# A two-layer decoder trunk on one core: projection units by halves of features, an earlier values product, and output pairs in another order

## The chip, the core and the metric

The kernel runs on one core of one Trainium2 chip, with float32 inputs and outputs. The metric is the time on the device in microseconds (us) of one execution. Its engines are TensorE (PE, matmuls), VectorE (DVE), ScalarE (ACT), GpSimd (POOL) and SyncE (SP, which issues the loads). Each engine works through its own instructions in order and waits where an operand isn't ready.

## The reference

The trunk has two layers over one sequence of 256 tokens with 1024 features. A layer is a half-step SwiGLU FFN, a token mixer and another half-step FFN; each reads a normed and modulated input and adds to x.

```python
def modulate(h, shift, scale):
    return h * (1 + scale[:, None, :]) + shift[:, None, :]
def hybrid_mixer(h, ...):
    proj = h @ w_in
    c_q, c_kv, k_pe, gate_b, gate_c, val = jnp.split(proj, offs, axis=-1)
    q = (rms_norm(c_q, q_a_norm) @ w_uq).reshape(B, S, N_HEADS, QK_NOPE_DIM + QK_ROPE_DIM)
    kv = (rms_norm(c_kv, kv_a_norm) @ w_ukv).reshape(B, S, N_HEADS, QK_NOPE_DIM + V_HEAD_DIM)
    ...
    attn = causal_attention(q_full, k_full, v).reshape(B, S, ATTN_WIDTH)
    conv = gate_b * causal_short_conv(gate_c * val, conv_w)
    merged = jnp.concatenate([rms_norm(attn, attn_out_norm), rms_norm(conv, conv_out_norm)], axis=-1)
    return merged @ w_o
for l in range(DEPTH):
    mod = jnp.split(c_act @ w_ada[l] + b_ada[l], N_MOD, axis=-1)
    h = modulate(rms_norm(x, ffn1_norm[l]), mod[0], mod[1])
    x = x + FFN_RESIDUAL * (1 + mod[2])[:, None, :] * swiglu(h, ffn1_w_gu[l], ffn1_w_down[l])
    h = modulate(rms_norm(x, mix_norm[l]), mod[3], mod[4])
    y = hybrid_mixer(h, ...)
    x = x + (1 + mod[5])[:, None, :] * y
    h = modulate(rms_norm(x, ffn2_norm[l]), mod[6], mod[7])
    x = x + FFN_RESIDUAL * (1 + mod[8])[:, None, :] * swiglu(h, ffn2_w_gu[l], ffn2_w_down[l])
return rms_norm(x, final_norm)
```

D_FF is 2816, the projection of the mixer has 2208 columns, there are 8 heads, and both groups (attention, convolution) are 512 wide.

## The kernel before

x lies on the chip, transposed: eight tiles x[0] to x[7] of 128 features by 256 tokens. A float32 product is made from three products of a shorter type: every operand is split into a high and a low part, and mm3 (line 287 is the line of all its matmuls) multiplies high by high, high by low and low by high. An mm3 is so three matmuls and takes one 128x128 weight tile and one feature tile.

**Weights** come as chunks of 1 MB (16 tiles of 128x128), in one fixed order on SP's queue. Each chunk has three buffers in rings of three: `raw` (the load), `hi` (ACT, line 262) and `lo` (DVE, line 265). In the mixer the splits go in four cuts of 128x512, in the FFNs in two of 128x1024. A load is issued when the `raw` buffer of three chunks ago has been split. Ahead of each chunk stand **modulation rows**, `ada`, of 0.5 MB each in a ring of four: one DVE instruction (line 189) reduces a row to one column of `mod`.

**Input of a sub-layer.** When a down projection, or the mixer's output, has finished an output tile m, DVE adds it to x[m] (`residual`, line 394, with a gate column from `mod`), and `put` scales it: ACT writes the high part of u[m] (line 351), DVE the low part (line 357), ACT squares x[m] (line 318) and DVE adds the square to `acc` (line 322). `shifts` splits the shift columns once eight of them are there. The norm's factor r comes later, from a sum over `acc` by a matmul with ones (`rstd`, lines 338 to 344), so products start on u before r is known and are scaled by r when they leave PSUM.

**The mixer** is a list of units, `ORDER`. K, Q, P (latents of kv, q and the rest), c (convolution) and d (its gate) are units of projection: a group of four units uses one chunk and one PSUM tile with two outputs, i = 0 and 1, over the eight features. In the kernel before, unit n of a group makes output n // 2 over features 0 to 3 (n even) or 4 to 7 (n odd). X is the sum for r; L, Z the latent norms; N, V, v the keys and values; q, s, t, a (0 to 3) are, for a pair of heads, queries, scores, the transposition of the probabilities, and the values product. n and m are the norms of the attention and of the convolution group; each ends in eight tiles `mr` that feed the output projection's halves A and B, of two chunks each (A0, A1, B0, B1). A unit w loads and splits the next chunk ahead of its use. B finishes pairs of output tiles (g, i odd); after each pair come residuals and puts for FFN2, whose first unit follows.

**What sets the order.** In the mixer PE and SP run as the list is written. For ACT and DVE a scheduler puts the instructions in an order by priority: `due(t)` sets it to a clock, which counts the matmuls emitted so far, plus t, and `SLACK` holds t for each kind of unit. A larger t puts the work later, if something else is ready. In the FFNs all engines go by this priority. `acc` in `out` is the pair of PSUM tiles of the output; `acc` in `Stat` the sum of squares.

Of the kernel before, what the change touches and what calls it, by code (L numbers as in the profile page):

```python
# [18 lines left out]
P = 128  # L19
L = 2  # L20
D = 1024
S = 256
KD = D // P
# [15 lines left out]
ENGS = {'p': mybir.EngineType.PE, 's': mybir.EngineType.SP, 'v': mybir.EngineType.DVE, 'a': mybir.EngineType.Activation}  # L39
MAN = 'sp'  # L40
SM_ACT = 2
ORDER = ("K K K X K Q Q P Q Q P P L c c c P c N Z V v q0 q1 s0 q2 c c c c t0 s1 a0 q3 c c c t1 c a1 s2 s3 c c c c t2 d d a2 t3 d d a3 "
         "d n w d w d d A A A w m A A w A A A B B B B B B B B").split()
WIN = dict(K=0, Q=1, P=2, c=3, d=7)
WO = dict(A=0, B=2)
SLACK = {'B': 6000, 'K': -2000, 'L': -4000, 'N': 0, 'P': 6000, 'Q': 0, 'V': 1000, 'X': 6000, 'Z': -4000, 'a': -4000, 'c': 6000, 'd': 0, 'm': 6000, 'n': 0, 'q': 2000, 's': -6000, 't': -4000}
CUTS = 4
GUARD = ('m',)
MIX_SPLIT, MIX_ADA = 2000, 2000
# [70 lines left out]
def trunk(ctx: ExitStack, tc, x_d, c_d, pos_d, small_d, cst_d, ada_d, gu1_d, dn1_d, win_d, up_d, wo_d, gu2_d, dn2_d, out_d):  # L120
# [25 lines left out]
    x = one.tile([P, KD, S], F32, name="x")  # L146
# [4 lines left out]
    uL, uH = u[:, :, 0:S], u[:, :, S:]  # L151
# [59 lines left out]
    for l in range(L):  # L211
# [4 lines left out]
        n = {}  # L216
# [64 lines left out]
    def due(t):  # L281

        tc.cur_priority = int(clock[0] + t)
# [75 lines left out]
    class Pre:  # L359
# [20 lines left out]
            nc.scalar.activation(hcol, sh, AF.Copy)  # L380
            nc.vector.tensor_tensor(lcol, sh, f32(hcol), ALU.subtract)

        def put(self, k):
            g = self.scale(k)
            hi_of(uH[:, k, :S], x[:, k, :], g)
            lo_of(uL[:, k, :], uH[:, k, :S], x[:, k, :], g)
            self.stat.add(x[:, k, :])


    def residual(src, m, l, sub, f, halves=False):  # L390
# [177 lines left out]
    def mixer(l, pre, nxt):  # L568
        mf = one.tile([P, NJ, S], F32, tag="aH", name=nm("mf"))
        mr = one.tile([P, NJ, S], F32R, tag="aL", name=nm("mr"))  # L570
        ckv, cq, conv, V, K = mf[:, 0:2], mf[:, 2:5], mf[:, 5:9], mf[:, 9:13], mf[:, 13:21]
# [32 lines left out]
        def proj(t, evac):  # L604

            n = seen[t] = seen.get(t, -1) + 1
            if n % 4 == 0:
                open_[t] = chunk(), ps_tile()
            w, pt = open_[t]
            i = n % 4 // 2  # L610
            for k in range(n % 2 * 4, n % 2 * 4 + 4):
                mm3(pt[:, i, :], w, i * KD + k, uH[:, k, :], uL[:, k, :], k == 0, k == KD - 1, 2)
            if n % 4 == 3:
                due(SLACK[t])
                evac(scaled(pt))
# [163 lines left out]
        def out(t):  # L779
            n = seen[t] = seen.get(t, -1) + 1  # L780
            half = "AB".index(t)
            zH, zL = ((atH, atL), (cvH, cvL))[half]
            g, i = divmod(n, 4)
            if not acc:
                acc.extend((ps_tile(), ps_tile()))
            if i == 0:
                open_[t] = chunk()
            w = open_[t]
            steps = [(m, i) for m in range(4)] if half == 0 else [(m, k) for k in range(i % 2 * 2, i % 2 * 2 + 2) for m in
                                                                  (i // 2 * 2, i // 2 * 2 + 1)]  # L790
            for m, k in steps:
                m += 4 * g
                dst = acc[m // 2 % 2][:, g, (m % 2) * S:(m % 2 + 1) * S]
                mm3(dst, w, m % 4 * 4 + k, zH[:, k, :], zL[:, k, :], half == 0 and k == 0 and m % 2 == 0, half == 1 and k == 3)
            if half == 1 and i % 2 == 1:
                due(SLACK["B"])
                for q in (i - 1, i):
                    m = 4 * g + q
                    residual(acc[m // 2 % 2][:, g, (m % 2) * S:(m % 2 + 1) * S], m, l, 1, 1.0)
                    nxt.put(m)  # L800
                    if m == 5:
                        nxt.shifts()

        do = dict(K=lambda: proj("K", kv_evac), Q=lambda: proj("Q", q_evac), P=lambda: proj("P", qk_evac),
                  c=lambda: proj("c", conv_evac), d=lambda: proj("d", gate_evac), X=lambda: pre.stat.rstd(r, t=SLACK["X"]), L=kv_norm, N=keys, Z=q_norm,
                  V=lambda: values(0), v=lambda: values(1), n=lambda: head_norm("n", sat, attn, O_AN, atH, atL),
# [97 lines left out]
def _layout(a):  # L904
    g = {}
    g["x"] = np.ascontiguousarray(a["x"][0].T.reshape(KD, P, S).transpose(1, 0, 2))
    g["c"] = np.ascontiguousarray(a["c"])
    g["pos"] = np.ascontiguousarray(np.broadcast_to(a["positions"][0].reshape(8, 32), (16, 8, 32)).reshape(P, 32))
    cols = []
    for l in range(L):  # L910
        for name in ("b_ada", "ffn1_norm", "mix_norm", "ffn2_norm", "q_a_norm", "kv_a_norm"):
            cols.append(a[name][l].reshape(-1, P).T)
        for j in range(3):
            cols.append(a["conv_w"][l, j].reshape(-1, P).T)
        for name in ("attn_out_norm", "conv_out_norm"):
            cols.append(a[name][l].reshape(-1, P).T)
    cols.append(a["final_norm"].reshape(-1, P).T)
    cols.append(_const_cols())
    g["small"] = np.ascontiguousarray(np.concatenate(cols, axis=1))
    g["cst"] = _consts()  # L920
    wt = a["w_ada"].transpose(0, 2, 1).reshape(L * NA, P, D)
    g["ada"] = np.ascontiguousarray(wt[[l * NA + t for l, t in ADA_ORDER]])
    for f in (1, 2):
        t = _tiles(a[f"ffn{f}_w_gu"]).reshape(L, KD, 2, NJ, P, P)
        w = t.transpose(0, 3, 4, 1, 2, 5).reshape(L, NJ, P, CH)
        if f == 1:
            head = w[0, :8].reshape(8, P, 8, 2, P).transpose(2, 1, 0, 3, 4).reshape(1, 8, P, CH)
            w = np.concatenate([np.concatenate([head, w[:1, 8:]], axis=1), w[1:]], axis=0)
        g[f"gu{f}"] = np.ascontiguousarray(w)
        t = _tiles(a[f"ffn{f}_w_down"]).transpose(0, 2, 1, 3, 4).reshape(L, 11, 16, P, P)  # L930
        g[f"dn{f}"] = np.ascontiguousarray(t.transpose(0, 1, 3, 2, 4).reshape(L, 11, P, CH))
    w = a["w_in"]
    kv, kpe, q = w[:, :, QR:QR + KVR], w[:, :, QR + KVR:QR + KVR + 32], w[:, :, :QR]
    sw = np.concatenate([kpe[:, :, 16:], kpe[:, :, :16]], axis=2)
    parts = [kv, q, sw, sw, kpe, kpe]
    o = QR + KVR + 32
    for i, s in [(i, s) for i in range(4) for s in (1, 2)] + [(i, 0) for i in range(4)]:
        parts.append(w[:, :, o + s * CW + i * P:o + s * CW + (i + 1) * P])
    t = _tiles(np.concatenate(parts, axis=2))
    t = t.transpose(0, 2, 1, 3, 4).reshape(L, 9, 16, P, P)  # L940
    g["win"] = np.ascontiguousarray(t.transpose(0, 1, 3, 2, 4).reshape(L, 9, P, CH))
    uk = a["w_ukv"].reshape(L, 2, P, H, 128)
    nope = uk[..., :64].reshape(L, 2, P, 4, P).transpose(0, 2, 3, 1, 4).reshape(L, P, 1024)
    v = uk[..., 64:].reshape(L, 2, P, 512).transpose(0, 2, 1, 3).reshape(L, P, 1024)
    uq = a["w_uq"].reshape(L, 3, P, H, 96)
    uq = np.concatenate([uq, uq[..., 80:96], uq[..., 64:80]], axis=-1)
    uq = uq.transpose(0, 2, 3, 1, 4).reshape(L, P, 24 * P)
    g["up"] = np.ascontiguousarray(np.concatenate([nope, v, uq], axis=2))
    t = _tiles(a["w_o"]).reshape(L, 2, 4, KD, P, P)
    t = t.transpose(0, 1, 3, 2, 4, 5).reshape(L, 4, 16, P, P)  # L950
    g["wo"] = np.ascontiguousarray(t.transpose(0, 1, 3, 2, 4).reshape(L, 4, P, CH))
    return g
# [21 lines left out]
```

## Time and profile before

| | |
|---|---|
| median of three runs | 999.11 us (999.49, 997.51, 999.11) |
| the profiled execution, its own time | 1002.27 us |
| its span, first to last instruction | 1000.5 us |
| mean granted clock of PE | 0.994 |
| PE busy | 977.1 us, 98% of the span |
| DVE busy | 854.1 us, 85% |
| ACT busy | 581.3 us, 58% |
| chain that ended last, share of PE | 78% |

Names of tiles are those of the program, without their numbers: `u` is the input of a sub-layer, `mf` and `mr` the mixer's tiles, `ps` a PSUM tile, `raw`, `hi`, `lo` a chunk. "SPq" is SP's DMA issue. A row of the timeline has the start, the duration, engine, line, operation, output <- inputs, shape and count; brackets hold the idle time ahead of it and what ended it.

### The profile page before, as it was taken

What the parts mean: (1) busy time and instruction counts of PE and PEld (TensorE: products, weight loads), DVE (VectorE), ACT (ScalarE), POOL (GpSimd) and SP (SyncE); (2) the same over time, 40 slices, a digit from 0 to 9 for tenths busy, and PEclk for the clock granted to TensorE, in tenths of its full rate; (3) what the DMA queues carried; (4) which work ended last, traced back from release to release, by engine and by line L of the source; (5) the groups of instructions that cost most, each with busy time, mean ns of one, the idle gap of its engine ahead of it and who ended that gap; (6) DMA issues with size and microseconds to landing.
All of it is one profiled execution on the core that took longest, in us unless ns stands there. A gap on an engine that the chain in (4) does not pass through costs nothing.

```text
span 1000.5 us, 16812 instructions
## 1 busy us (share of the span) xinstructions
PE 977.1 (98%) x6560; PEld 898.1 (90%) x6560; DVE 854.1 (85%) x1598; ACT 581.3 (58%) x1010; POOL 8.0 (1%) x27
## 2 busy tenths in 40 slices
PE   9999999999999999999999999998999999999996
PEld 7999998899989988888998888888998998888885
DVE  5899999999999998988899878877799999766653
ACT  4465544467856755654486555543687676656541
POOL 0000110000000000000000000000000000000000
PEclk9999999999999999999999999998999999999998
DMA  9999998874746687877768777776355547655531
GB/s 348 376 361 340 336 320 324 311 282 154 275 178 253 234 318 253 301 267 291 270 219 324 279 258 283 277 255 214 124 217 193 200 171 290 215 178 201 173 122 43
DMA packets 47007, 250.78 MB, mean 251 GB/s; under 512 B 5504, under 2 KB 5824, under 8 KB 26576
## 3 DMA queue, kind: packets, MB, share of 16 engines
q1 hardware_dynamic: 46224, 248.81, 68.3%
q8 instruction: 51, 0.84, 0.3%
q10 hardware_dynamic: 288, 0.65, 0.2%
q0 software_dynamic: 416, 0.25, 0.1%
q14 instruction: 28, 0.23, 0.1%
HBM read 248.59 MB, written 1.10 MB: 250 GB/s over the span
## 4 chain that ended last, share of the span: by engine, by line
PE 78%; DVE 11%; DMA 7%; issue 1%; ACT 1%; SPq 0%; DVEq 0%; ACTq 0%
PE ps L287 78%; DMA ada<-in_ada 6%; DVE lo L265 5%; DVE ada L189 1%; DVE x L394 1%; DMA raw<-in_gu 1%; DVE acc L322 1%; DVE u L357 1%; PE ps L731 1%; DVE mr L355 1%; ACT hi L262 0%; DMA cb<-in_c 0%; DVE nt L594 0%; ACT mr L351 0%; DVE mf L767 0%
## 5 line engine op out<-in xcount | busy, mean ns | idle before, releaser
L287 PE MATMUL ps<-u,hi 128*128 128x256 f32 (+2 forms) x2464 | 599.8, 324 | 6.5 <-ACT u L351 3.7
L287 PE MATMUL ps<-u,lo 128*128 128x256 f32 (+1 forms) x1664 | 470.1, 283 | 1.1 <-DVE lo L265 1.1
L287 PEld LDWEIGHTS ps<-u,hi 128*128 128x128 f32 x2464 | 413.5, 190 | 46.4 <-ACT u L351 4.3
L265 DVE TENSOR_TENSOR lo<-raw,hi 128x1024 fp32r<-128x1024 f32 (+2 forms) x384 | 394.8, 1046 | 41.4 <-ACT hi L262 40.9
L262 ACT ACTIVATE hi<-raw 128x1024 fp32r<-128x1024 f32 (+2 forms) x384 | 338.3, 912 | 113.4 <-PE ps L287 48.9
L287 PEld LDWEIGHTS ps<-u,lo 128*128 128x128 f32 x1664 | 315.9, 190 | 1.4 <-DVE lo L265 1.4
L287 PE MATMUL ps<-a,hi 128*128 128x512 f32 (+1 forms) x792 | 248.6, 372 | 1.4 <-DVE a L355 1.4
L189 DVE CUSTOM_DVE_ANT_0 ada<-ada,cb,small 128x1024 f32<-128x1024 f32 x144 | 183.1, 1280 | 33.4 <-DMA ada<-in_ada 32.8
L287 PE MATMUL ps<-a,lo 128*128 128x256 f32 x704 | 197.9, 281 | 0.0
L287 PEld LDWEIGHTS ps<-a,hi 128*128 128x128 f32 x792 | 143.0, 189 | 29.8 <-DVE a L355 1.7
L287 PEld LDWEIGHTS ps<-a,lo 128*128 128x128 f32 x704 | 133.2, 189 | 0.0
L351 ACT ACTIVATE a<-cc 128x256 fp32r<-128x256 f32 x88 | 36.3, 415 | 68.0 <-DVE cc L413 56.3
L287 PE MATMUL ps<-mr,hi 128*128 128x256 f32 x384 | 70.6, 285 | 0.0
L351 ACT ACTIVATE u<-x,gs 128x256 fp32r<-128x256 f32 x40 | 20.3, 507 | 84.6 <-DVE x L394 84.6
L287 PEld LDWEIGHTS ps<-mr,hi 128*128 128x128 f32 x384 | 60.2, 192 | 0.8 <-issue 0.3
L287 PE MATMUL ps<-mr,lo 128*128 128x256 f32 x192 | 54.3, 283 | 0.0
L394 DVE SCALAR_TENSOR_TENSOR x<-ps,gate,x 128x256 f32<-128x256 f32 x76 | 35.9, 480 | 19.2 <-PE ps L287 18.5
L355 DVE TENSOR_TENSOR a<-cc,a 128x256 fp32r<-128x256 f32 x88 | 37.0, 422 | 16.0 <-ACT a L351 15.8
L412 ACT ACTIVATE cc<-g 128x256 f32<-128x256 f32 x54 | 22.5, 418 | 41.5 <-DVE g L411 41.5
L411 DVE TENSOR_TENSOR g<-ps,g 128x512 f32<-128x512 f32 x54 | 37.0, 685 | 0.7 <-ACT g L410 0.6
L287 PEld LDWEIGHTS ps<-mr,lo 128*128 128x128 f32 x192 | 36.8, 191 | 0.0
L410 ACT ACTIVATE g<-ps 128x512 f32<-128x512 f32 x54 | 31.2, 578 | 0.0
(121 smaller groups left out, 568.4 us busy)
## 6 DMA issues: line engine op xcount, KB each, us to landing
raw<-in_gu SPq DMA_DIRECT2D x87, 1024.0 KB, 5.8
ada<-in_ada SPq DMA_DIRECT2D x144, 512.0 KB, 6.2
raw<-in_dn SPq DMA_DIRECT2D x44, 1024.0 KB, 5.2
raw<-in_win SPq DMA_DIRECT2D x18, 1024.0 KB, 5.7
raw<-in_wo SPq DMA_DIRECT2D x8, 1024.0 KB, 4.8
raw<-in_up SPq DMA_DIRECT2D x2, 1024.0 KB, 5.9
raw<-in_up SPq DMA_DIRECT2D x2, 768.0 KB, 4.4
raw<-in_up SPq DMA_DIRECT2D x4, 384.0 KB, 3.1
```

What stands on the lines that cost most here:

```text
L189: nc.vector.tensor_tensor_reduce(out=a, in0=a, in1=cb, scale=1.0, scalar=sm(l, t), op0=ALU.mult, op1=ALU.add, accum_out=mods[l][:, t:t + 1])
L262: nc.scalar.activation(hi[:, zs[q]], raw[:, zs[q]], AF.Copy)
L265: nc.vector.tensor_tensor(lo[:, zs[q]], raw[:, zs[q]], f32(hi[:, zs[q]]), ALU.subtract)
L287: nc.tensor.matmul(dst, a, b, **kw)
L322: nc.vector.tensor_tensor(self.acc, self.acc, t, ALU.add)
L351: nc.scalar.activation(dH, src, AF.Copy, scale=scale)
L355: nc.vector.tensor_tensor(dL, src, f32(dH), ALU.subtract)
L357: nc.vector.scalar_tensor_tensor(dL, src, scale, f32(dH), ALU.mult, ALU.subtract)
L394: nc.vector.scalar_tensor_tensor(x[:, m, :], s, g, x[:, m, :], ALU.mult, ALU.add)
L410: nc.scalar.activation(t2, pg[:, :, :S], AF.Copy)
L411: nc.vector.tensor_tensor(t2, pg[:, :, S:], t2, ALU.add)
L412: nc.scalar.activation(sg, t2[:, 0, :], AF.Silu)
```

## The change

It has three parts.

1. **Projection by halves of features.** Unit n of a group now makes output n % 2 over features 0 to 3 (n = 0, 1) or 4 to 7 (n = 2, 3). The weights are rearranged on the host so that cut n of the chunk is still the one that unit n uses. The list begins K K Q Q K X K Q Q, where it began K K K X K Q Q P Q Q.
2. **The last values product** a3 moves ahead of a gate unit: t3 d a3 d d n in place of t3 d d a3 d n. The unit w that followed n and d, the first of four early loads, is left out; three remain, so that chunk B1 is taken when it is used.
3. **Output pairs.** Both residuals of a pair come first, then both scalings and splits, then the shifts (after the third pair), and last, with a due time of their own (`y`, 5000), the squares and their sum. `SLACK` of B goes from 6000 to 1500, and to 0 for the last pair.

```diff
-ORDER = ("K K K X K Q Q P Q Q P P L c c c P c N Z V v q0 q1 s0 q2 c c c c t0 s1 a0 q3 c c c t1 c a1 s2 s3 c c c c t2 d d a2 t3 d d a3 "
-         "d n w d w d d A A A w m A A w A A A B B B B B B B B").split()
+ORDER = ("K K Q Q K X K Q Q P P P L c c c P c N Z V v q0 q1 s0 q2 c c c c t0 s1 a0 q3 c c c t1 c a1 s2 s3 c c c c t2 d d a2 t3 d a3 "
+         "d d n d w d d A A A w m A A w A A A B B B B B B B B").split()
-SLACK = {'B': 6000, ...
+SLACK = {'B': 1500, 'y': 5000, ...
-        def put(self, k):
+        def put(self, k, add=True):
             g = self.scale(k)
             hi_of(uH[:, k, :S], x[:, k, :], g)
             lo_of(uL[:, k, :], uH[:, k, :S], x[:, k, :], g)
-            self.stat.add(x[:, k, :])
+            if add:
+                self.stat.add(x[:, k, :])
...
-            i = n % 4 // 2
-            for k in range(n % 2 * 4, n % 2 * 4 + 4):
-                mm3(pt[:, i, :], w, i * KD + k, uH[:, k, :], uL[:, k, :], k == 0, k == KD - 1, 2)
+            i, h = n % 2, n % 4 // 2
+            for k in range(4 * h, 4 * h + 4):
+                mm3(pt[:, i, :], w, 4 * (n % 4) + k % 4, uH[:, k, :], uL[:, k, :], k == 0, k == KD - 1, 2)
...
-                due(SLACK["B"])
-                for q in (i - 1, i):
-                    m = 4 * g + q
+                pair = 4 * g + i - 1, 4 * g + i
+                due(SLACK["B"] if n < 7 else 0)
+                for m in pair:
                     residual(acc[m // 2 % 2][:, g, (m % 2) * S:(m % 2 + 1) * S], m, l, 1, 1.0)
-                    nxt.put(m)
-                    if m == 5:
-                        nxt.shifts()
+                for m in pair:
+                    nxt.put(m, False)
+                if n == 5:
+                    nxt.shifts()
+                due(SLACK["y"])
+                for m in pair:
+                    nxt.stat.add(x[:, m, :])
...
-    t = t.transpose(0, 2, 1, 3, 4).reshape(L, 9, 16, P, P)
+    t = t.transpose(0, 2, 1, 3, 4).reshape(L, 9, 2, 2, 4, P, P).swapaxes(2, 3).reshape(L, 9, 16, P, P)
```

How the instructions stand on an engine, in three places.

PE at the entry of layer 1's mixer, before: ps_7331 is FFN1's last output tile, hi_7425 and lo_7426 are K's chunk, ps_7439 its output. Twelve mm3 (three units) of K stand before the sum over acc_6909 into ps_7476.

```order
L287 MATMUL ps_7331<-a_5563,lo_7352 128x256
L287 MATMUL ps_7439<-u,hi_7425 128x258
L287 MATMUL ps_7439<-u,hi_7425 128x256
L287 MATMUL ps_7439<-u,lo_7426 128x258
...
L287 MATMUL ps_7476<-acc_6909,ones 128x256
```

The same place in the changed kernel: ps_7476 is now Q's output, hi_7465 and lo_7466 its chunk, and the sum goes to ps_7513.

```order
L287 MATMUL ps_7331<-a_5563,lo_7352 128x256
L287 MATMUL ps_7439<-u,hi_7425 128x258
L287 MATMUL ps_7439<-u,hi_7425 128x256
L287 MATMUL ps_7439<-u,lo_7426 128x258
...
L287 MATMUL ps_7476<-u,hi_7465 128x258
L287 MATMUL ps_7476<-u,hi_7465 128x256
L287 MATMUL ps_7476<-u,lo_7466 128x258
...
L287 MATMUL ps_7439<-u,hi_7425 128x258
...
L287 MATMUL ps_7513<-acc_6909,ones 128x256
```

Two units of Q (24 matmuls) now stand between K's second and third unit, and the sum comes after K's third, the fifth unit in all.

DVE around the attention norm of layer 0, before: acc_2911 is the norm's sum of squares, acc_3243 the convolution's; lo_3338 the second chunk (A1) of the output projection; ps_3173 the first two gate tiles.

```order
L189 ISA ada_3426,mod_88<-ada_3426,cb,small 128x1024
L189 ISA mod_88 128x1
L762 SCALAR_TENSOR_TENSOR mf_2298<-cpad_3146,small,mf_2298 128x256
L585 TENSOR_REDUCE pb_3238<-ps_3173 128x2
L586 TENSOR_TENSOR g_392_3239<-ps_3173,r_2300 128x512
L265 TENSOR_TENSOR lo_3338<-raw_3336,hi_3337 128x512
L767 SCALAR_TENSOR_TENSOR mf_2298<-g_392_3239,pb_3238,mf_2298 128x256 x2
L265 TENSOR_TENSOR lo_3338<-raw_3336,hi_3337 128x512 x2
L322 TENSOR_TENSOR acc_2911<-acc_2911,sq_3254 128x256
L322 TENSOR_TENSOR acc_3243<-acc_3243,sq_3246 128x256
L265 TENSOR_TENSOR lo_3338<-raw_3336,hi_3337 128x512
L342 SCALAR_TENSOR_TENSOR rs_a_3287<-rs_y_3285 128x256
```

And in the changed kernel, where the chunk is lo_3412:

```order
L763 SCALAR_TENSOR_TENSOR mf_2298<-cpad_3146,small,mf_2298 128x256
L322 TENSOR_TENSOR acc_2911<-acc_2911,sq_3231 128x256
L586 TENSOR_REDUCE pb_3246<-ps_3173 128x2
L587 TENSOR_TENSOR g_393_3247<-ps_3173,r_2300 128x512
L265 TENSOR_TENSOR lo_3412<-raw_3410,hi_3411 128x512
L768 SCALAR_TENSOR_TENSOR mf_2298<-g_393_3247,pb_3246,mf_2298 128x256 x2
L265 TENSOR_TENSOR lo_3412<-raw_3410,hi_3411 128x512
L322 TENSOR_TENSOR acc_3251<-acc_3251,sq_3254 128x256
L342 SCALAR_TENSOR_TENSOR rs_a_3287<-rs_y_3285 128x256
L265 TENSOR_TENSOR lo_3412<-raw_3410,hi_3411 128x512
L343 TENSOR_TENSOR rs_a_3287<-rs_a_3287,rs_me_3286 128x256
L265 TENSOR_TENSOR lo_3412<-raw_3410,hi_3411 128x512
```

The last addition to acc_2911 moves ahead of the gate's evacuation, a modulation row leaves, and cuts of A1 stand between the steps of the reciprocal (one behind each of its first two).

ACT from the end of the convolution norm of layer 0 to the third put of FFN2, before: hi_3489 is B1, hi_3710 and hi_3820 are FFN2's first two chunks.

```order
L351 ACTIVATE mr_2299<-nt_3460 128x256
L262 ACTIVATE hi_3489<-raw_3488 128x512 x4
L262 ACTIVATE hi_3710<-raw_3709 128x1024 x2
L351 ACTIVATE u<-x,gs_92 128x256
L318 ACTIVATE acc_3566<-x 128x256
L351 ACTIVATE u<-x,gs_92 128x256
L318 ACTIVATE sq_3574<-x 128x256
L262 ACTIVATE hi_3820<-raw_3819 128x1024 x2
L351 ACTIVATE u<-x,gs_92 128x256
L318 ACTIVATE sq_3607<-x 128x256
L351 ACTIVATE u<-x,gs_92 128x256
L318 ACTIVATE sq_3616<-x 128x256
```

And in the changed kernel, where hi_3474 is B0 and hi_3608 is B1:

```order
L262 ACTIVATE hi_3474<-raw_3473 128x512 x4
L262 ACTIVATE hi_3608<-raw_3607 128x512 x4
L262 ACTIVATE hi_3710<-raw_3709 128x1024
L380 ACTIVATE u<-mod_88 128x8
L262 ACTIVATE hi_3710<-raw_3709 128x1024
L351 ACTIVATE u<-x,gs_92 128x256
L318 ACTIVATE acc_3560<-x 128x256
L351 ACTIVATE u<-x,gs_92 128x256
L318 ACTIVATE sq_3562<-x 128x256
L262 ACTIVATE hi_3820<-raw_3819 128x1024
L351 ACTIVATE u<-x,gs_92 128x256 x2
L318 ACTIVATE sq_3601<-x 128x256
```

B0's splits are now behind the convolution norm's tiles too, and for the second pair both scalings stand ahead of the squares.

More of the change, by code (lines that the diff above doesn't have):

```diff
@@ L41 @@
 SM_ACT = 2
-ORDER = ("K K K X K Q Q P Q Q P P L c c c P c N Z V v q0 q1 s0 q2 c c c c t0 s1 a0 q3 c c c t1 c a1 s2 s3 c c c c t2 d d a2 t3 d d a3 "
-         "d n w d w d d A A A w m A A w A A A B B B B B B B B").split()
+ORDER = ("K K Q Q K X K Q Q P P P L c c c P c N Z V v q0 q1 s0 q2 c c c c t0 s1 a0 q3 c c c t1 c a1 s2 s3 c c c c t2 d d a2 t3 d a3 "
+         "d d n d w d d A A A w m A A w A A A B B B B B B B B").split()
 WIN = dict(K=0, Q=1, P=2, c=3, d=7)
 WO = dict(A=0, B=2)
-SLACK = {'B': 6000, 'K': -2000, 'L': -4000, 'N': 0, 'P': 6000, 'Q': 0, 'V': 1000, 'X': 6000, 'Z': -4000, 'a': -4000, 'c': 6000, 'd': 0, 'm': 6000, 'n': 0, 'q': 2000, 's': -6000, 't': -4000}
+SLACK = {'B': 1500, 'y': 5000, 'K': -2000, 'L': -4000, 'N': 0, 'P': 6000, 'Q': 0, 'V': 1000, 'X': 6000, 'Z': -4000, 'a': -4000, 'c': 6000, 'd': 0, 'm': 6000, 'n': 0, 'q': 2000, 's': -6000, 't': -4000}
 CUTS = 4
```

## The prediction

> **What bounds the kernel now.** I began with the page's busy times and the view of waits, each grouped over the whole span.
>
> ```profile
> PE 977.1 (98%) x6560; PEld 898.1 (90%) x6560; DVE 854.1 (85%) x1598; ACT 581.3 (58%) x1010; POOL 8.0 (1%) x27
> PE ps L287 <- ACT u L351: 3.7, 3, 2.6
> PE ps L287 <- DVE acc L322: 3.3, 4, 1.5
> PE ps L287 <- DVE u L357: 2.7, 3, 1.0
> PE ps L287 <- DVE lo L265: 1.1, 1, 1.1
> ```
>
> TensorE (PE) is busy for 977.1 of 1000.5 us, and the change removes no matmul, so only three things can be won: waits of PE, time in which matmuls run slowly, and time that a wait costs without being shown. The wait rows name few causes (total, times, longest): features of the normed input u, norm sums (acc), and one weight split (lo). The timeline of PE tells where these lie; the bracket is the idle time ahead of the instruction and what ended it.
>
> ```profile
> 206.99 0.39 PE L287 MATMUL ps<-u,lo 128*128 128x258 f32 x1 [1.14 <-DVE lo L265]
> 283.29 0.67 PE L287 MATMUL ps<-acc,ones 128*128 128x256 f32 x2 [1.47 <-DVE acc L322]
> 317.15 0.38 PE L287 MATMUL ps<-u,hi 128*128 128x258 f32 x1 [0.41 <-ACT u L351]
> 318.53 0.38 PE L287 MATMUL ps<-u,hi 128*128 128x256 f32 x1 [1.00 <-DVE u L357]
> 694.73 0.39 PE L287 MATMUL ps<-u,hi 128*128 128x258 f32 x1 [2.59 <-ACT u L351]
> 695.78 0.58 PE L287 MATMUL ps<-u,hi 128*128 128x256 f32 x1 [0.67 <-DVE u L357]
> 772.41 0.67 PE L287 MATMUL ps<-acc,ones 128*128 128x256 f32 x2 [1.47 <-DVE acc L322]
> ```
>
> The places are: the entry of the mixer (206.99 in layer 0, 694.73 and 695.78 in layer 1), the sum of the attention group's norm (283.29, 772.41), and the entry of FFN2 behind the mixer (317.15, 318.53, with like waits in layer 1). All three parts of the change act at exactly these places. Behind the longest wait stands a second loss, which the windows around it show (length, PE busy with its matmuls, granted clock, DMA share, GB/s):
>
> ```profile
> 695.80:701.70 5.90, 5.90 (x25) 0.50 0.43 133
> 701.70:705.00 3.30, 3.30 (x29) 0.97 0.00 0
> 284.00:300.00 16.00, 15.81 (x130) 1.00 0.55 198
> ```
>
> After the wait PE ran for 5.90 us at half the clock. At full clock a matmul takes 16.00 / 130 = 0.12 us (one unit of the projection, 12 matmuls, takes 1.44); half of 5.90 us, 2.95, was lost. The 1.47-us wait at 283.29 was followed by a clock of 1.00.
>
> **Part 1, the projection by halves of features.** Why layer 1 waits is read from the rows of the queues around it.
>
> ```profile
> 685.29 1.01 SPq L180 DMA_DIRECT2D ada<-in_ada  x1
> 687.20 2.50 DVE L265 TENSOR_TENSOR lo<-raw,hi 128x512 fp32r<-128x512 f32 x4
> 689.46 0.41 PE L287 MATMUL ps<-u,hi 128*128 128x258 f32 x2
> 692.44 1.28 DVE L189 CUSTOM_DVE_ANT_0 ada<-ada,cb,small 128x1024 f32<-128x1024 f32 x1 [2.74 <-DMA ada<-in_ada]
> 693.65 0.48 DVE L394 SCALAR_TENSOR_TENSOR x<-ps,gate,x 128x256 f32<-128x256 f32 x1
> 694.16 0.51 ACT L351 ACTIVATE u<-x,gs 128x256 fp32r<-128x256 f32 x1 [3.42 <-DVE x L394]
> 695.25 0.48 DVE L357 SCALAR_TENSOR_TENSOR u<-x,gs,u 128x256 fp32r<-128x256 f32 x1
> 695.64 0.42 DVE L322 TENSOR_TENSOR acc<-acc,sq 128x256 f32<-128x256 f32 x1
> ```
>
> A modulation row, issued at 685.29, held VectorE (DVE) until 692.44; the last residual stands behind it, so the high part of u[7] came at 694.67 and the low part at 695.73. PE began K at 689.46 and needs u[7] as the eighth of sixteen feature steps of 0.36: from 689.46 + 7 × 0.36 = 691.98. In the new order K and Q each run their first two units, features 0 to 3 of both outputs. That is 4 × 1.44 = 5.76 us, to 695.22, and then three more steps (features 4, 5, 6) come, to 696.30. Both parts of u[7] are there 0.57 us before. Q's weights are no new wait: the eight lo cuts of K and Q end with the four of 687.20, at 689.70, and Q begins at 692.34. The norm sum, now behind five units, is due at 689.46 + 7.20 = 696.66, and its last addend is ready at 696.06. So 2.59 + 0.67 = **3.26 us of waits go**, and with them the cause of the **2.95 us** at half clock. Next late would be that sum, by 0.6 us of spare time. What it releases, r and then K's evacuation, comes two units later in the order of work than before; K's tile has its last unit only at 698.1 now, and its reader L lies eleven units in, at 705.3, some 7 us for an evacuation.
>
> The Trainium skill's page "TensorE: Matmul & The Clock Gate" (Part 1, "What's actually happening") has the clock fall to half after an idle window of about 3.4 us and rise after as long a busy one, the window running free, so that it differs between runs. This trace agrees that a 3.26-us pair of waits halves the clock and 1.47 does not; by the page the loss would be an estimated 1.7 us, the row has 2.95, and the row decides.
>
> In layer 0 the wait at 206.99 is for another thing.
>
> ```profile
> 206.24 1.29 DVE L265 TENSOR_TENSOR lo<-raw,hi 128x512 fp32r<-128x512 f32 x2
> 208.19 3.69 DVE L265 TENSOR_TENSOR lo<-raw,hi 128x512 fp32r<-128x512 f32 x6
> ```
>
> The first lo cut of K ends only at 206.9, behind the last residual; DVE's order there stays as it was, so the 1.14 stays. Of the six cuts from 208.19 two are K's; Q's first ends near 208.19 + 3 × 0.615 = 210.0, and PE, released at 206.99, now wants it two units (2.9 us) later, near 209.8: **+0.2 us** (bounds 0 and +0.8, if each of Q's cuts is a step late; a cut feeds four feature steps, 1.44 us of PE for 0.615 of DVE, so it does not add up).
>
> **Part 2, the last values product a unit earlier.**
>
> ```profile
> 276.76 0.80 ACT L734 ACTIVATE pT<-ps 128x768 f32<-128x768 f32 x1
> 279.32 0.88 PE L287 MATMUL ps<-pT,mf 128*64 128x256 f32 x8
> 280.36 0.36 ACT L747 ACTIVATE mf<-ps 128x256 f32<-128x256 f32 x1
> 281.98 0.71 ACT L318 ACTIVATE sq<-mf 128x256 f32<-128x256 f32 x2
> 282.72 0.76 DVE L322 TENSOR_TENSOR acc<-acc,sq 128x256 f32<-128x256 f32 x2
> 286.92 0.82 DVE L355 TENSOR_TENSOR mr<-nt,mr 128x256 fp32r<-128x256 f32 x2
> 288.11 0.40 PE L287 MATMUL ps<-mr,hi 128*128 128x256 f32 x2
> ```
>
> The product moves from 279.32 to 277.88, and the transposed weights it needs (pT) are ready at 277.56: 0.32 to spare. The copy followed it by 1.04, so it is at 278.92; copy 0.36, square 0.36, addition 0.38 give 280.0, or 281.2 if the two splits that stood between copy and square stay there. The sum's place is 283.29 - 1.47 = 281.82, since three units and the product still lie ahead of it: the 1.47 goes. But the three units behind it now cover less. Before, from sum to first A there were 288.11 - 283.29 = 4.82 us, and mr[0] was ready after 4.04 (286.92 + 0.41 less 283.29), 0.78 early. In the new order two more lo cuts of about 0.62 stand between the steps of the reciprocal on DVE, and the rs_y of ScalarE (ACT) waits behind A1's splits and two squares of the gate: between 0 and 2 us of delay, of which I take 1.4 (both cuts and a little), 0.6 after the cover. That makes 1.47 - 0.6 = **-0.9 us in each layer, -1.8 in all** (bounds -2.9 and +0.5).
>
> **Part 3, the output pairs, and one early load less.**
>
> ```profile
> raw<-in_gu SPq DMA_DIRECT2D x87, 1024.0 KB, 5.8
> 293.99 0.33 SPq L252 DMA_DIRECT2D raw<-in_gu  x1
> 312.02 0.41 PE L287 MATMUL ps<-u,hi 128*128 128x258 f32 x2
> 318.00 0.48 DVE L357 SCALAR_TENSOR_TENSOR u<-x,gs,u 128x256 fp32r<-128x256 f32 x1
> 319.46 1.28 DVE L189 CUSTOM_DVE_ANT_0 ada<-ada,cb,small 128x1024 f32<-128x1024 f32 x1
> 319.97 0.59 PE L287 MATMUL ps<-acc,ones 128*128 128x256 f32 x2
> ```
>
> FFN2's first block, 48 matmuls, takes 319.97 - 312.02 = 7.95 us instead of 5.8: 2.1 us are lost, since u[6] is cut at 318.00 where PE wants it at 315.5. The new order puts both residuals first and moves the additions of squares back, which frees DVE of some five of 0.4 ahead of the last pair: u[6] near 316.2 to 316.8. Against it, chunk B0's four lo cuts (4 × 0.62 = 2.5) now lie behind the convolution norm's chain instead of before it; two modulation rows (2 × 1.28) leave the same stretch, like that of 319.46, which falls behind the sum. The sum then waits for the square of x[7], 318.5 to 319.1 behind its u: a loss of 1.7 to 2.35 where there were 2.1. I take **-0.3 in each layer, -0.6 in all** (bounds -1.3 and +0.3 each). The load of the second FFN2 chunk, issued at 293.99, needs the buffer that B0's cuts free, near 301.4 now; with 5.8 to land it comes at 307.2, before ACT needs it for the split that stands ahead of the third u, about 308. That cover is the thinnest of this part.
>
> **The sum.** Against the profiled execution (1002.27): -3.26 - 2.95 + 0.2 - 1.8 - 0.6 = -8.4, 993.9. That execution lies 3.16 above the median of the runs shown (999.11), which is nearly the 2.95 of the half clock; I read that as a loss of this execution that the timed runs mostly do not have. Then 999.11 - 3.26 + 0.2 - 1.8 - 0.6 = **993.6 us**.
>
> **Rivals.**
> 1. *The half clock is in every run.* For it: it follows the wait directly, and the wait comes from the fixed order. Against it: the offset of 3.16. The time would be 993.6 - 2.95 = 990.7. Chance 0.17; my forecast 0.47.
> 2. *The modulation row lands early in the timed runs, so that there is no layer-1 wait to win.* Its 692.44 - 685.29 = 7.15 us stand against a median of 6.2 in the page's row of these loads:
>
> ```profile
> ada<-in_ada SPq DMA_DIRECT2D x144, 512.0 KB, 6.2
> ```
>
> That is 0.95 of the 3.26 at the median; all of it needs a landing after 3.4 us (u[7] by 691.98 instead of 695.73). With all of it gone, 999.11 + 0.2 - 2.4 = 996.9; chance 0.18, mostly not with the whole.
> 3. *The entry's wait is pushed back, not removed.* The spare time for u[7] is 0.57 us, and moves to the Q and K weights or a later row would put some 1 to 2 us back: 995.1. Chance 0.11. In layer 0 the change does not do what its words say at all, which is in the sum.
> 4. *Slower.* The dropped load makes the exit late: the second chunk's load waits for B0's cuts, ACT, which takes its work in order, stands at its split, and u[2] to u[7] come behind it. From a landing near 308.0 each further us is a us of PE. To outweigh the gains of 5.5 us, it must cost 2.8 us in each layer, a landing at 310.8, 9.4 us after issue instead of 5.8. With 4 us in each layer the time is 993.6 + 8 = 1001.6. Against it: the median of 87 such loads is 5.8, and only two of the loads stand at this place. Chance 0.07.
>
> **How the numbers follow.** About 0.2% (2 us) is what a measurement of this kernel can tell from no change, so "same" is 997.1 to 1001.1. My forecast, rival 1 and rival 3 (0.75 together) are faster, and so is somewhat over half of rival 2, with 996.9 close to the bound: 0.11 of 0.18. Of rival 4 0.05 is slower, the rest same. Faster 0.83, same 0.11, slower 0.06 (a little for what I do not see). The range of the forecast alone, by the bounds of parts 2 and 3, is 991 to 996. With rival 1 at its lower and rival 2 at its upper end it is 990.0 to 997.9.
>
> **What would show it.** In the changed profile: at the layer-1 entry no wait over 0.5 us between K's first matmul and the norm sum, with u[7]'s low part done before the third step of K's third unit, and a granted clock of 1.00 for the 12 us behind it; at the layer-0 entry still about 1.1 us on lo; no wait at the sum of the attention norm, and instead up to 1 us at the first A matmul; at FFN2's first block 7.4 to 8.2 us from its first matmul to the sum. I am wrong if FFN2's first block takes over 10 us (rival 4), or if a wait of 2 us or more for u or lo stands anywhere in the first ten units of layer 1.

## The result, and the profile after

The changed kernel takes 991.71 us (median of 21 runs, 990.43 to 999.11) against 1000.0 us before (median of 21 runs beside them, 994.27 to 1004.86). The ratio is 0.9936, with a 95% interval of 0.9918 to 0.9954: 6.4 us faster, 4.6 to 8.2. The profiled execution has a span of 989.3 us where the one before had 1000.5. The forecast of 993.6 us is 1.9 off and the direction holds; most of this text is about how little of the gain came from the term that was to bring it.

The waits of PE in the changed kernel, grouped (total, times, longest):

```profile
PE ps L287 <- DVE lo L265: 1.1, 1, 1.1
PE ps L287 <- DVE acc L322: 1.1, 2, 0.6
PE ps L287 <- DVE u L355: 1.1, 1, 1.1
...
PE ps L287 <- ACT mr L351: 0.5, 2, 0.3
```

And where they lie, from PE's timeline:

```profile
206.78 0.39 PE L287 MATMUL ps<-u,lo 128*128 128x258 f32 x1 [1.14 <-DVE lo L265]
286.88 0.84 PE L287 MATMUL ps<-mr,hi 128*128 128x256 f32 x2 [0.26 <-ACT mr L351]
317.91 0.70 PE L287 MATMUL ps<-acc,ones 128*128 128x256 f32 x2 [0.61 <-DVE acc L322]
336.95 0.47 PE L287 MATMUL ps<-u,hi 128*128 128x512 f32 x1 [1.11 <-DVE u L355]
798.00 0.70 PE L287 MATMUL ps<-acc,ones 128*128 128x256 f32 x2 [0.52 <-DVE acc L322]
```

The waits for u at layer 1's mixer and at both FFN2 entries are gone, and so are the 1.47 at the norm's sums; 0.26 stands at the first A, the 1.14 at layer 0's mixer is unchanged. New are the waits at FFN2's sums (0.61 and 0.52) and the one at 336.95. Behind layer 1's entry the clock stays full (length, PE busy, granted clock, DMA share, GB/s):

```profile
690.00:700.00 10.00, 10.00 (x84) 1.00 0.26 80
700.00:710.00 10.00, 10.00 (x84) 1.00 0.58 197
```

DVE's rows there, though, warn against reading the two traces as cause and effect:

```profile
685.55 1.28 DVE L189 CUSTOM_DVE_ANT_0 ada<-ada,cb,small 128x1024 f32<-128x1024 f32 x1 [0.86 <-DMA ada<-in_ada]
687.35 0.48 DVE L395 SCALAR_TENSOR_TENSOR x<-ps,gate,x 128x256 f32<-128x256 f32 x1 [0.51 <-PE ps L287]
689.16 0.48 DVE L357 SCALAR_TENSOR_TENSOR u<-x,gs,u 128x256 fp32r<-128x256 f32 x1
```

The modulation row was done by 686.8, and the last residual waited for PE, not for the row. PE began K at 687.1, and the old order would have wanted u[7] by 687.1 + 2.52 = 689.6, which is when it came. In this execution there was nothing to cover.

The span cut into stages, by the start of the first matmul of each in PE's timeline (lengths in us; the runs are explained below):

| stage | before | whole change | e1: part 1 | e2: part 2 | e3: part 3 | c2: load kept |
|---|---|---|---|---|---|---|
| mixer 0, K to keys | 25.3 | 25.5 | 25.5 | 25.3 | 25.3 | 25.5 |
| keys to attention norm's sum, each layer | 52.6 | 50.9 | 52.6 | 50.9 | 52.6 | 50.9 |
| sum to first A, each layer | 4.8 | 5.2 | 4.8 | 5.2 | 4.8 | 5.2 |
| FFN2's first block, layer 0 / 1 | 8.0 / 7.9 | 6.5 / 6.4 | 8.0 / 8.8 | 8.6 / 8.8 | 5.7 / 5.7 | 5.7 / 5.7 |
| rest of FFN2's 22 blocks, 0 / 1 | 118.7 / 118.7 | 120.1 / 118.8 | 118.7 / 119.4 | 119.9 / 119.7 | 118.7 / 118.7 | 118.7 / 118.7 |
| down projection of layer 1's FFN1 | 64.0 | 62.3 | 66.2 | 68.1 | 62.3 | 61.6 |
| mixer 1, K to keys | 30.4 | 23.9 | 23.9 | 23.9 | 25.8 | 23.9 |

### The profile page after: what moved, and what is told of

The parts are those of the page before. It is cut to its first block, busy times and chain, and to the rows that moved or that the text cites. A ratio compares the mean times of both kernels' runs of the same rounds, so it can differ in the third digit from the quotient of the medians.

```text
span 989.3 us, 16826 instructions
## 1 busy us (share of the span) xinstructions
PE 974.2 (98%) x6560; PEld 895.6 (91%) x6560; DVE 852.8 (86%) x1598; ACT 581.8 (59%) x1010; POOL 8.0 (1%) x27
## 4 chain that ended last, share of the span: by engine, by line
PE 90%; DVE 6%; DMA 1%; ACT 1%; issue 1%; DVEq 0%; ACTq 0%
PE ps L287 89%; DVE lo L265 2%; DMA raw<-in_gu 1%; DVE ada L189 1%; PE ps L732 1%; DMA x<-in_x 0%; DVE acc L322 0%; DVE u L357 0%; ACT hi L262 0%; DVE x L395 0%; PE ps L443 0%; DVE nt L595 0%; DVE mr L355 0%; DVE rs_a L343 0%; DVE rs_a L342 0%
```

## The experiments

First theory, that of the prediction: a modulation row that lands late holds the last residual at layer 1's entry, and part 1 covers that; this is most of the gain. Rival: that wait was an accident of one execution, and the gain is from elsewhere. Four kernels, each the kernel before with one thing changed.

**e1, part 1 alone.**

```diff
-ORDER = ("K K K X K Q Q P Q Q P P L ...
+ORDER = ("K K Q Q K X K Q Q P P P L ...
...
-            i = n % 4 // 2
+            i, h = n % 2, n % 4 // 2
...
```

> Part 1 alone on the kernel before. Theory of the held row: a modulation row that lands late stands on DVE ahead of the last residual of layer 1's entry, in most executions, and the order by halves covers it. Then this run is 4 to 7 us faster than before (the 3.26 us of waits, and more or less of the 2.95 us at half clock), no wait over 0.5 us stands at layer 1's entry, and layer 0's entry still waits about 1.1 us for lo. Rival, an accident of the one profiled execution: within 1.5 us of before, since the timed runs had no such wait.

Measured: 995.77 us (12 runs, 993.8 to 1001.73) beside 997.33 before (31 runs, 993.7 to 1004.48), ratio 0.9985 [0.996, 1.001]: -1.5 us, from -4 to +1. The entry has no wait (mixer 1 takes 23.9), and yet the 4 to 7 us did not come. The row was late here too: it held DVE until 695.3, where PE had begun K at 692.7, and u[7]'s high part came 3.6 us after K's begin. In e3 below, with the old order, 3.3 us gave waits of 0.69 and 0.67, so part 1 covered an estimated 1.7 us in this execution. The profiled execution lost its time elsewhere, at the begin of FFN1's down projection and at FFN2's entry:

```profile
636.21 0.50 PE L287 MATMUL ps<-a,hi 128*128 128x512 f32 x1 [2.12 <-DVE a L355]
803.18 0.38 PE L287 MATMUL ps<-u,hi 128*128 128x258 f32 x1 [0.69 <-ACT u L351]
804.56 0.38 PE L287 MATMUL ps<-u,hi 128*128 128x256 f32 x1 [1.00 <-DVE u L357]
800.00:810.00 10.00, 8.32 (x53) 0.83 0.75 260
```

**e2, part 2 alone.**

```diff
-... t3 d d a3 d n w d w d d A ...
+... t3 d a3 d d n d w d d A ...
```

> Part 2 alone (a3 a unit earlier, the first early load left out). Both theories: the 1.47-us wait at the attention norm's sum goes in both layers, a wait of 0.2 to 0.7 appears at the first A; 1 to 2.5 us faster in all. At layer 1's entry the old order stands, so a wait for u of 0 to 4 us is to be seen again if the theory of the held row is right, as long as the row is late in this execution.

Measured: 1000.55 us (12 runs, 994.88 to 1005.01), ratio 1.0013 [0.9984, 1.0041]: no gain. The sum's wait went, as expected, but FFN2's first block grew from 8.0 to 8.6 and from 7.9 to 8.8. At layer 1's entry there was no wait in this execution, in the old order: PE had been held 3.93 us before, so the row had its time.

```profile
317.24 0.39 PE L287 MATMUL ps<-u,hi 128*128 128x258 f32 x1 [0.98 <-ACT u L351]
638.65 0.79 PE L287 MATMUL ps<-a,hi 128*128 128x512 f32 x1 [3.93 <-DVE a L355]
693.17 1.29 DVE L189 CUSTOM_DVE_ANT_0 ada<-ada,cb,small 128x1024 f32<-128x1024 f32 x1 [0.43 <-DMA ada<-in_ada]
695.40 0.48 DVE L394 SCALAR_TENSOR_TENSOR x<-ps,gate,x 128x256 f32<-128x256 f32 x1 [0.94 <-PE ps L287]
```

**e3, part 3 alone.**

```diff
-SLACK = {'B': 6000, ...
+SLACK = {'B': 1500, 'y': 5000, ...
...
-                due(SLACK["B"])
+                due(SLACK["B"] if n < 7 else 0)
...
+                for m in pair:
+                    nxt.put(m, False)
...
+                due(SLACK["y"])
+                for m in pair:
+                    nxt.stat.add(x[:, m, :])
```

> Part 3 alone (residuals of a pair first, squares last). If the 1.5 us that FFN2's first block gained in each layer come from the order of the pairs, its time from the first matmul to the sum is 6.3 to 6.7 us here, and the run is up to 3 us faster; layer 0 may give it back later as it did in the changed kernel. If they come from the load left out, the block takes 7.5 to 8 us as before and the run is within 1 us of before.

Measured: 990.61 us (8 runs, 988.96 to 995.96), ratio 0.9921 [0.989, 0.9952]: -7.9 us, from -11 to -4.8, a gain as large as the whole change's, from the part that I had priced at 0.6. FFN2's first block takes 5.7 us in both layers, its 48 matmuls at 0.12 without a wait. The low parts of u[6] and u[7] on DVE in layer 0, where FFN2 began at 312.4:

```profile
314.66 0.48 DVE L357 SCALAR_TENSOR_TENSOR u<-x,gs,u 128x256 fp32r<-128x256 f32 x1
315.07 0.42 DVE L322 TENSOR_TENSOR acc<-acc,sq 128x256 f32<-128x256 f32 x1
315.40 0.48 DVE L357 SCALAR_TENSOR_TENSOR u<-x,gs,u 128x256 fp32r<-128x256 f32 x1
```

u[6] is cut 2.3 us after FFN2's begin, where it had been 318.00 - 312.02 = 6.0. In this execution the old order of the projection did wait for u[7], 0.69 and 0.67 us, with the clock staying at 1.00:

```profile
689.27 0.39 PE L287 MATMUL ps<-u,hi 128*128 128x258 f32 x1 [0.69 <-ACT u L351]
690.33 0.39 PE L287 MATMUL ps<-u,hi 128*128 128x256 f32 x1 [0.67 <-DVE u L357]
```

**e5, one row behind the last residual.** The kernel before; only the reduction of the row that held the residual moves, by an order constraint on DVE. In the two traces PE, ACT and SP have the same order, and DVE's differs in this row alone.

```diff
-                for q in guard:
+                for q in guard + (tail if i in (36, 119) else []):
                     es.enter_context(tc.issue_after(q))
                 ada(ada_target(i + 1))
```

> The kernel before, with one modulation row's reduction on DVE (the one that held the last residual at layer 1's entry) put behind that residual, its split and its square; nothing else moves on any engine. Theory of the held row: the waits for u[7] at layer 1's entry go although the old order of the projection stands, and the run is 3 to 6 us faster than before, about what part 1 alone gives. Rival (the wait is u[7]'s own chain, or the load of weights): the wait stays, within 1 us of before.

Measured: 996.65 us (12 runs, 992.88 to 1000.38), ratio 0.9982 [0.9959, 1.0006]: -1.8 us, from -4 to +0.6. No wait at the entry, and the gain of e1, as the theory says of two cures of one ill; but by the two ratios the ill is worth one to two microseconds in the mean, not six, and both intervals include zero. The theory of the mechanism stands, its price falls.

The first theory now says: the entry's wait is real but changes from run to run, and part 3 carries the gain. Its rival on the mechanism: rows and loads set the pace there anyway, so that PE's wait at the entry hardly reaches the end. It is settled by making the last residual late in both orders, with five copies that nobody reads ahead of it on DVE.

```diff
+                if l == 1 and sub == 0 and m == KD - 1:
+                    idle = work([P, S], "nt", 2)
+                    for _ in range(5):
+                        nc.vector.tensor_copy(idle, ps[:, :S])
                 residual(ps, m, l, sub, 0.5, m < KD - 1)
```

**c3, old order of the projection with part 3 (e3), made late.**

> Part 3 alone (so the old order of the projection), with five copies of 128x256 that nobody reads ahead of layer 1's last residual on DVE; three cuts of P's split move ahead of it with them, which makes u[7] some 3.2 us late. Theory of the entry: PE waits 3 to 4.5 us for u[7], half the clock follows for some 6 us, and the run is 4 to 7 us slower than part 3 alone. Rival, the wait there hardly reaches the end (rows and loads set the pace): under 2 us slower.

Measured: 996.61 us (10 runs, 993.31 to 999.57), 6.0 over e3's median (on another chip; the kernel before had 997.39 beside this run and 997.33 beside e3). PE's timeline, and two windows:

```profile
692.39 1.10 PE L287 MATMUL ps<-u,hi 128*128 128x258 f32 x2 [5.02 <-ACT u L351]
692.40:695.00 2.60, 2.60 (x10) 0.50 0.61 156
695.00:697.00 2.00, 2.00 (x9) 0.50 0.46 190
```

**c4, parts 1 and 3 (c1 below), made late by the same copies.**

> Parts 1 and 3 with the same five copies ahead of layer 1's last residual. Theory of the entry: u[7] is needed only after 19 feature steps, 6.8 us from K's begin, and comes at about 5.7, so there is no wait over 0.7 us and no half clock, and the run is within 1 us of parts 1 and 3 without the copies. Rival (the halves do not cover a late residual, the weights or r take over): 2 us or more slower.

Measured: 990.86 us (7 runs, 989.1 to 994.29), 1.0 over c1's median. PE began K at 686.14, u[7] was cut as late as 691.5, 5.4 us behind, and PE was not idle once in the windows around:

```profile
691.00 0.49 DVE L357 SCALAR_TENSOR_TENSOR u<-x,gs,u 128x256 fp32r<-128x256 f32 x1
680.00:690.00 10.00, 10.00 (x86) 1.00 0.71 258
690.00:700.00 10.00, 10.00 (x85) 1.00 0.26 80
```

So part 1 does what its order says: the copies cost the old order 6 us and the new one about 1, which is within the intervals of c1 and c4 (0.9923 [0.9898, 0.9948] and 0.9933 [0.991, 0.9955]). It is an insurance, paid with 0.2 us in layer 0.

Next, part 2. The whole change (991.71) was no faster than part 3 alone.

**c1, the whole change without part 2.**

> The changed kernel without part 2 (parts 1 and 3 alone). From the stages: part 3 alone took 5.7 us for FFN2's first block in both layers, with part 2 it is 6.5 and layer 0 loses another 1.4 later; part 2 gains 1.7 and loses 0.9 to 1.0 up to FFN2. Theory, part 2 is worth nothing or less beside part 3: 989 to 991 us, as fast as the whole change or up to 2 us faster. Rival, the parts add up and part 2 gives its 1.5 us: 1 to 2 us slower than the whole change, 992 to 994.

Measured: 989.82 us (6 runs, 988.76 to 993.69), ratio 0.9923 [0.9898, 0.9948]: as fast as the whole or up to 2 us faster. FFN2's first block takes 5.7 in both layers. Its profiled execution, the longest of the six, waited where e1 and e2 did:

```profile
633.25 0.50 PE L287 MATMUL ps<-a,hi 128*128 128x512 f32 x1 [1.84 <-DVE a L355]
```

**c2, the whole change with the early load kept.** Part 2 has two edits: the product a unit earlier, and one w less. This puts the w back.

```diff
-... t3 d a3 d d n d w d d A ...
+... t3 d a3 d d n w d w d d A ...
```

> The changed kernel with the early load that part 2 left out put back behind n; the last values product stays a unit earlier. Theory, the load left out is what costs: FFN2's first block takes 5.7 to 5.9 us, layer 0's rest of FFN2 118.7, the norm's sum still has no wait, and the run is 1.5 to 3 us faster than the whole change (988 to 990). Rival, the shorter way from the sum to the first A is what costs: the block and the rest stay at 6.5 and 120, within 1 us of the whole change.

Measured: 988.1 us (6 runs, 987.71 to 993.64), ratio 0.9917 [0.9889, 0.9944]; run again as **d4**, beside the whole change on one chip, 988.8 (6 runs, 986.78 to 992.72), where the whole change, **d3**, had 993.36 (12 runs, 990.41 to 998.23).

> The whole change once more, beside the next run on the same chip: 990.4 to 992 in most runs.

> The changed kernel with the early load kept, once more beside the whole change: 987.7 to 988.5 in most runs, 2 to 3.5 us faster than it, if the load left out is what costs; no difference if the session made it.

Four of d4's six runs are under 989, no run of the whole change is under 990.4. It beats both kernels: ratio to before 0.9905 [0.9873, 0.9937]. Both expectations were missed in size: only five of d3's twelve runs are at 992 or below, and the medians lie 4.6 us apart, not 2 to 3.5. What the missing load cost is seen in layer 0. With the load kept the mixer takes a modulation row at 277.74 on DVE and FFN2's first 25 us two (319.50 and 321.04); in the whole change the mixer lacks that row and FFN2's beginning has three (318.98, 327.13, 334.84). The last of them stands on DVE shortly ahead of the splits of u that PE then waits for at 336.95:

```profile
334.84 1.28 DVE L189 CUSTOM_DVE_ANT_0 ada<-ada,cb,small 128x1024 f32<-128x1024 f32 x1
...
336.38 1.43 DVE L355 TENSOR_TENSOR u<-qh,u 128x256 fp32r<-128x256 f32 x4
```

With the load kept the same splits begin on DVE 3.7 us earlier (3.4 counted from FFN2's begin), and u[6] and u[7] of FFN2's entry are cut by 313.9 (FFN2 begins at 311.1) instead of 316.05 (311.4):

```profile
313.44 0.48 DVE L357 SCALAR_TENSOR_TENSOR u<-x,gs,u 128x256 fp32r<-128x256 f32 x1
332.70 1.09 DVE L355 TENSOR_TENSOR u<-qh,u 128x256 fp32r<-128x256 f32 x3
```

Last, the wait at the begin of layer 1's down projection, which came in some executions of almost any version (1.39, 2.12, 3.93, 1.09, 1.84 in before, e1, e2, e5, c1; none in the others). Its DVE rows stand behind modulation rows that wait for their DMA, so I moved eight rows out of that FFN into the mixer behind it.

```diff
-PACE = ..., (84, 97), (117, 130), (133, 136), ...
+PACE = ..., (84, 97), (117, 122), (133, 136), ...
```

**d1, c2 with these rows moved, and d2, the kernel before with them moved.**

> The changed kernel with the early load kept, and eight of the modulation rows that are loaded during layer 1's FFN1 moved into the mixer behind it (five rows instead of thirteen over the last twelve... that is 25 rows instead of 33 over its 33 chunks). Theory, rows and chunks together set the pace there and now and then make PE wait at the begin of the down projection: that stage takes 61.6 to 62.3 us, and all runs lie within 1.5 us of the fastest, 987.5 to 989. Rival, the mixer cannot take eight more rows: waits for rows or for splits there, 1 to 4 us slower.

> The kernel before with the same eight rows moved from layer 1's FFN1 into its mixer, and nothing else. Theory, rows set the pace: no wait at the begin of FFN1's down projection and, since the row that held the last residual comes with less ahead of it, a shorter wait or none at the mixer's entry; 994 to 995.5 us, with a spread of 2 instead of 10 us. Rival, the spread comes from elsewhere (the FFN2 entry and the clock behind it): within 1 us of before with the same spread.

Measured: d1 990.15 us (6 runs, 989.63 to 991.08); d2 998.23 us (12 runs, 996.55 to 1000.47), ratio 1.001 [0.9989, 1.003]. The spread fell as expected, from 5.9 (c2) to 1.5 us and from 10.7 (before, 23 runs) to 3.9, and the down projection begins without a wait; the times expected, 987.5 to 989 and 994 to 995.5, did not come. The mixer did not take the rows for nothing: in layer 1 the first A waits instead, in d1 with the clock falling to 0.83 in the window behind the waits' begin:

```profile
765.14 0.38 PE L287 MATMUL ps<-mr,hi 128*128 128x256 f32 x1 [0.91 <-ACT mr L351]
766.21 0.38 PE L287 MATMUL ps<-mr,hi 128*128 128x256 f32 x1 [0.69 <-DVE mr L355]
760.00:770.00 10.00, 8.40 (x56) 0.83 0.52 197
```

In d2 that wait is 1.95 us. So the rows' pace has a part in the spread. This way of relieving it gains nothing: the medians lie 1.4 us above those of d4 and of before on the same chip, with intervals that overlap.

## Why the prediction was right, and where its terms were not

The sum was -3.26 + 0.2 - 1.8 - 0.6 = -5.5 against the median of 999.11; measured are -6.4 [-8.2, -4.6]. The total fits by luck: part 1 gave less than its term and part 3 more, and the two errors offset each other.

**Part 1, the entry.** The mechanism holds: the row held the residual (e5), and 19 feature steps cover what 7 do not (c3 against c4). The size is wrong. "That makes 3.26 us of waits go" took one execution's wait for every run's. In the profiled executions of the old order (before, e2, e3, d2) the two waits came to 3.26, 0, 1.36 and 0.90, a mean of 1.4, and part 1 alone gave 1.5 us (-1 to 4). In the nine profiled executions in which rows and residual keep their places (before, the changed kernel and d3, e1, e2, e3, c1, c2, d4) the row held the residual for 2 to 4 us behind K's begin in five (before, e1, e3, c2, d3) and was done in time in four. Rival 2, the row early in the timed runs, is nearer to the truth for this term. The 2.95 us at half clock were rightly kept out of the sum: in e3 and d2 the clock stayed at 1.00 behind these waits. Layer 0's entry came as worked out: 1.14 unchanged, +0.2 for Q's cuts (25.3 to 25.5).

**Part 2, the norm's sum.** To FFN2's begin it is right, in part by luck: -1.6 at the sum and +0.4 instead of +0.6 at the first A, but +0.6 and +0.4, for which there was no term, from there to FFN2. That makes -0.7 and -0.9 against the -0.9 of the sum. What I did not carry further is the load left out. I put it into part 3 as a trade of four cuts (2.5) for two rows (2.6) on DVE, even. It is not even: FFN2's first block is 0.8 and 0.7 us longer than with part 3 alone, and a row that leaves the mixer comes back in FFN2, where the rest of layer 0's takes 1.4 us longer. So part 2 as a whole gives nothing (e2, 1.0013), and its first edit alone gives about 2 us (c2 against c1: 988.1 and 989.82, intervals that overlap).

**Part 3, the exit.** "I take -0.3 in each layer" is the term that failed. Alone it gains 2.2 us in each layer in FFN2's first block; in the whole change 1.4 and 1.5. The bound was -1.3. The step at fault is what leaves DVE's way: "some five of 0.4 ahead of the last pair", additions of squares. Between B's first residual and the low part of u[6] DVE made five additions before, and five in the changed kernel, in both layers; e3 has four. What leaves is the splitting of FFN2's own weights, which the prediction did not count. Layer 0 before:

```profile
308.78 1.22 DVE L265 TENSOR_TENSOR lo<-raw,hi 128x1024 fp32r<-128x1024 f32 x1
311.83 1.22 DVE L265 TENSOR_TENSOR lo<-raw,hi 128x1024 fp32r<-128x1024 f32 x1
314.21 1.22 DVE L265 TENSOR_TENSOR lo<-raw,hi 128x1024 fp32r<-128x1024 f32 x1
316.87 1.22 DVE L265 TENSOR_TENSOR lo<-raw,hi 128x1024 fp32r<-128x1024 f32 x1
```

And in e3:

```profile
309.33 1.21 DVE L265 TENSOR_TENSOR lo<-raw,hi 128x1024 fp32r<-128x1024 f32 x1
316.13 1.22 DVE L265 TENSOR_TENSOR lo<-raw,hi 128x1024 fp32r<-128x1024 f32 x1
317.60 1.22 DVE L265 TENSOR_TENSOR lo<-raw,hi 128x1024 fp32r<-128x1024 f32 x1
318.81 1.22 DVE L265 TENSOR_TENSOR lo<-raw,hi 128x1024 fp32r<-128x1024 f32 x1
```

Before, four such cuts stand ahead of u[6] at 318.00; in e3 one does, with u[6] at 314.66. Three cuts and an addition, each taking 1.14 and 0.34 us of DVE's time in a row of such work, make 3.8 us, and u[6] comes 3.7 us earlier, 2.3 instead of 6.0 after FFN2's begin. In the changed kernel three such cuts and a smaller one stay ahead of it, the modulation row that stood there is gone and the first residual comes 0.9 us sooner. All this fits the lower due time of B, which puts residuals and scalings ahead of the cuts. No run has the due time without the new order in a pair, so which of the two does it is argued, not shown. The changed kernel's rows:

```profile
315.17 0.88 DVE L357 SCALAR_TENSOR_TENSOR u<-x,gs,u 128x256 fp32r<-128x256 f32 x2
...
317.44 0.42 DVE L322 TENSOR_TENSOR acc<-acc,sq 128x256 f32<-128x256 f32 x1
```

I had u[6] at 316.2 to 316.8 and the last addition at 318.5 to 319.1, with FFN2's begin at 312.02. It began at 311.37; counted from there both came 0.4 to 1.0 us sooner than that. A second effect had no term: the old entry's waits, 0.69 and 1.00, sometimes halve the clock (mean 0.83 in e1 and e5, 800 to 810), which takes another 1.6 us then (e1: 8.8 - 7.9 in the first block and 119.4 - 118.7 in the rest). Of the ten FFN2 entries in the profiles without part 3 (before, e1, e2, e5, d2) five lose clock so. Twice 2.2 us of waits, and 1.6 us in half of the entries, make an estimated 6 of e3's 7.9 us [4.8, 11]; the rest is not traced to a stage.

**The rivals.** Rival 4, slower by a late exit, did not come, but its cause, the load left out, did cost time (c2 and d4 against the whole change). Rival 3 did not come. Rival 1, the clock in every run, fell, since the wait that it hangs on isn't in every run. The mean granted clock of the timed runs of before was 0.9954 (31 runs, 0.992 to 0.997), of the changed kernel 0.9968 (0.9957 in d3), of c2 the second time 0.9973; it differs from run to run.

**The marks I named.** Entry without wait, clock 1.00, 1.1 at layer 0, no wait at the sum, under 1 us at the first A: all there. FFN2's first block, 7.4 to 8.2 expected, took 6.4 to 6.5. That mark alone would have shown the wrong split.

**Open.** Why one execution has rows late and another not is not shown; up to the chunk loads 50 us into layer 1's FFN1 the issue times of eight of the kernels, counted from that FFN's begin, agree within 0.1 us for several loads in a row, and they part from there with the DMA's landing times. In the first comparison the changed kernel's median lies 8.3 us under that of before, in the third 3.5 (993.36 and 996.87, ratio 0.9957 [0.9933, 0.998]); part of that may be such luck. Against the later medians of before (997.33, 997.39, 996.87) the 999.11 that the forecast started from was high.

## What to carry to other kernels

A wait in one profile is the wait of one execution: before its whole length goes into a sum, ask what the waiting thing hangs on. One that ends with a DMA's landing varies; one that ends with another engine's work of fixed order (the wait for u[6] at FFN2's entry was 0.99 to 1.06 us in both layers of all five profiles without part 3) was there every time, and is the surer gain. Where an engine in order prepares the next stage's operands, list everything that stands ahead of the one that stage waits for: here the weight cuts of that stage counted for more than the sums of squares that I had in mind. And if an early load is dropped, follow its splits and everything that they push back up to the stage in which they end.

## What was unexpected about the hardware

The clock can fall after less idleness than I had thought, and not every time. Waits of 0.69 and 0.99 us close to each other halved it in e5 about a microsecond after PE had gone on, while before had the same two waits in layer 1 (0.69 and 1.00) and a clock of 1.00. The rows and windows of e5, then those of before:

```profile
799.37 0.38 PE L288 MATMUL ps<-u,hi 128*128 128x258 f32 x1 [0.69 <-ACT u L352]
800.75 0.38 PE L288 MATMUL ps<-u,hi 128*128 128x256 f32 x1 [0.99 <-DVE u L358]
799.00:800.80 1.80, 0.43 (x2) 1.00 1.01 405
800.80:802.50 1.70, 1.70 (x12) 0.80 0.72 198
802.50:803.50 1.00, 1.00 (x4) 0.50 0.94 377
```

```profile
806.44 0.38 PE L287 MATMUL ps<-u,hi 128*128 128x258 f32 x1 [0.69 <-ACT u L351]
807.82 0.38 PE L287 MATMUL ps<-u,hi 128*128 128x256 f32 x1 [1.00 <-DVE u L357]
800.00:810.00 10.00, 8.32 (x66) 1.00 0.59 203
```

The Trainium skill's page "TensorE: Matmul & The Clock Gate" (Part 1, "What's actually happening") puts the fall after an idle window of about 3.4 us that runs free. Nor were the 2.59 and 0.67 us at layer 1's mixer in before one idle stretch, since a matmul stands between them. That the same waits end both ways agrees with a free-running window; that 1.7 us of idleness are enough does not agree with a window that has to be idle throughout, and the measurement decides.
